# Channel mixing moved ahead of the norm's scale and the pooling, with one load of the input in pairs of chunks

## The chip, the cores and the metric

The kernel runs on one core of one Trainium2 chip. The metric is the device time of one execution in microseconds; before the change it was 927.83 us, the median of 3 runs (927.12 to 928.20). The profile is of one execution of its own, 927.41 us as timed; its span, from the first to the last recorded instruction, is 925.5 us. Engines are named as in the profile: PE (TensorE, matmul), DVE (VectorE), ACT (ScalarE), POOL (GpSimd), SP (SyncE, which issues nearly all loads).

## The reference

A trunk of two layers on 512 tokens with 1024 channels, in float32. Layer 0 mixes tokens by causal pooling, layer 1 by sliding-window attention; each mixer is followed by a gated MLP with a causal convolution of width 3. Only the pooling mixer of layer 0 is touched:

```
def pool_mixer(h, w, b, scale):            # h = rms_norm(x, norm_mix[0])
    ...
    for gi, win in enumerate(POOL_WINDOWS):      # 2, 4, 8, 16
        sl = slice(gi * POOL_GC, (gi + 1) * POOL_GC)   # 256 channels each
        ...
        mean = (c - lo) / count[None, :, None]   # causal mean over win tokens
        outs.append(mean - hf[..., sl])
    p = jnp.stack(outs, axis=2).astype(h.dtype)
    y = jnp.einsum('bsgc,gcd->bsgd', p, w) + b   # one 256x256 matrix per group
    return y.reshape(B, S, D) * scale
...
h = h + pool_mixer(rms_norm(h, norm_mix[0]), ...)
hn = rms_norm(h, norm_ffn[0])
h = h + conv_glu_ffn(hn, ...)
```

Pooling acts on tokens and the 256x256 matrix on channels, so the two commute; the norm's per-channel weight can be folded into the matrix, and its per-token factor r0 can be put on either side of the matrix, but must stand before the pooling.

## The kernel before

The channels lie in NC = 8 chunks of P = 128 partitions, the S = 512 tokens along the free dimension, in NT = 4 tiles of 128. The stream is the eight tiles h[c] (128x512); the f0x tiles are its chunks for the MLP, scaled with that norm's weight. Matrix products keep float32 accuracy by splitting each operand into two float32r parts, h (rounded, by ACT) and l (the rest, by DVE or, for weights called with the engine G, by POOL in quarters of 256 columns). `mm3` makes three matmuls of one product: h by h, l by h, h by l (L84, L85, L86). The eight PSUM banks hold 512 float32 columns each.

`pool_mixer` ran in this order. x came twice. First by tokens (`xt`, 4 loads of 512 KB): ACT squares each token tile and sums it along the row, a short chain on ACT and DVE makes the factor r0 of these tokens, DVE scales a band matrix (128 x 144 columns: the pooling window of a token tile and its spill into the next) with it, and eight plain float32 matmuls (L299) pool the eight channel chunks, straight from `xt`. Then, for every chunk in turn, `mixed` (m) evicts the pooled bank as two float32r parts, `product` (p) multiplies with the mixing matrix (six matmuls with 512 columns), `bias` (b) adds a per-channel bias to h[c], which came transposed in a second set of eight loads, `total` (t) adds the product to h[c] on DVE, and `normed` (n) makes f0x of it: the rounded part on ACT, the rest on DVE (`split_scaled`, L258 and L259). `early_weights` (w) splits the first four tiles of the MLP's input matrix.

A string `order` sets in which sequence these steps are issued; the instructions marked `pin` keep that sequence on their engine. Each engine works its queue strictly in order, and an instruction that waits holds up those behind it. PE's queue has all pooling, then all products, then the MLP.

The MLP (`mlp_in`) starts with two weight tiles together: for each chunk k six matmuls, three for each tile, 48 in all, then the second pair of tiles the same way, then one tile at a time. All that follows is the same in both kernels.

Of the kernel before, what the change touches and what calls it, by code (L numbers as in the profile page):

```python
# [19 lines left out]
F32 = mybir.dt.float32  # L20
F32R = mybir.dt.float32r
# [36 lines left out]
def trunk(ctx: ExitStack, tc: tile.TileContext, x_tok, x_t, vecs, w_pool, w_kq, w_v, w_o, w_in, w_out, out_a, out_b):  # L58
# [10 lines left out]
    def small(pool, n, words, dt=F32, **kw):  # L69
        return pool.tile([P, words], dt, **kw)[:, :n]  # L70
# [72 lines left out]
    xt = fst.tile([P, NT, D], F32, name="xt")  # L143
    for i in range(NT):
        nc.sync.dma_start(xt[:, i, :], x_tok[i * P : (i + 1) * P, :])
    vec = small(cst, NV, -(-NV // 64) * 64, name="vec")
    wpool_raw = [fst.tile([P, 1024], F32, name=f"wpool{g}_raw") for g in range(2)]
    for g in range(2):
        nc.sync.dma_start(wpool_raw[g], w_pool[:, g * 1024 : (g + 1) * 1024])
# [9 lines left out]


# [3 lines left out]
    band = fst.tile([P, 8, BW], F32, name="band")  # L164
    def edge_copy(g):
        a = WINDOWS[g] - 1
        pin(V.tensor_copy(band[:, 4 + g, a:], band[:, g, a:]))

    for g, w in enumerate(WINDOWS):
        b = band[:, g, :]  # L170
        V.memset(b, 1.0 / w)
        G.affine_select(b, b, [[1, BW]], ALU.is_ge, 0.0, base=0, channel_multiplier=-1)
        G.affine_select(b, b, [[-1, BW]], ALU.is_ge, 0.0, base=w - 1, channel_multiplier=1)
        G.affine_select(b, b, [[1, BW]], ALU.not_equal, 1.0 / w - 1.0, base=0, channel_multiplier=-1)
        f = band[:, 4 + g, : w - 1]
        G.affine_select(f, rc[:, : w - 1], [[1, w - 1]], ALU.is_ge, 0.0, base=0, channel_multiplier=-1)
        G.tensor_tensor(f, f, ident[:, : w - 1], ALU.subtract)
        if g < 2:
            edge_copy(g)
    ones = cst.tile([P, P], F32, name="ones")  # L180
    G.memset(ones, 1.0)


    def rsqrt_mean(dst, ssq, n, root=False):
# [7 lines left out]
        if root:  # L192
            A.activation(y, ssq, AF.Sqrt, bias=eps, scale=1.0 / D)
# [68 lines left out]

    def pool_mixer(norm, xs, ws):
        r0 = small(fst, NT, 32, name="r0")
        ss0 = small(fst, 2 * NT, 32, name="ss0")

        warm = small(fst, BW, 192, name="warm")
        V.memset(warm, 0.0)
        for i in range(12):
            T.matmul(banks[-1][:, :BW], lhsT=warm[:, :P], rhs=warm, start=True, stop=True)  # L270
        for i in range(NT):

            cut = D // 2 if i == 0 else D
            junk = fst.tile([P, D], F32, tag="junk", name=f"junk{i}")
            if cut < D:
                pin(
                    V.tensor_tensor_reduce(
                        out=junk[:, cut:],
                        in0=xt[:, i, cut:],
                        in1=xt[:, i, cut:],  # L280
                        scale=1.0,
                        scalar=0.0,
                        op0=ALU.mult,
                        op1=ALU.add,
                        accum_out=ss0[:, NT : NT + 1],
                    )
                )
            A.activation(junk[:, :cut], xt[:, i, :cut], AF.Square, accum_out=ss0[:, i : i + 1])
            if cut < D:
                pin(V.tensor_tensor(ss0[:, i : i + 1], ss0[:, i : i + 1], ss0[:, NT : NT + 1], ALU.add))  # L290
                for g in (2, 3):
                    edge_copy(g)
            rsqrt_mean(r0[:, i : i + 1], ss0[:, i : i + 1], 1, root=True)
            n = min(BW, S - i * P)
            sband = fst.tile([P, 4, BW], F32, tag="sband", name=f"sband{i}", bufs=2)
            e = 0 if i else 4
            pin(V.tensor_scalar(sband[:, :, :n], band[:, e : e + 4, :n], r0[:, i : i + 1], None, ALU.mult))
            for c in range(NC):
                T.matmul(  # L299
                    banks[c][:, i * P : i * P + n],  # L300
                    lhsT=xt[:, i, c * P : (c + 1) * P],
                    rhs=sband[:, c // 2, :n],
                    start=(i == 0),
                    stop=(i == NT - 1),
                    skip_group_check=True,
                )
        wpool = []
        for g in range(4):
            raw = wpool_raw[g // 2][:, (g % 2) * 512 : (g % 2 + 1) * 512]
            hh = fst.tile([P, 512], F32R, name=f"wpool{g}_h")  # L310
            ll = fst.tile([P, 512], F32R, name=f"wpool{g}_l")
            A.activation(hh, raw, AF.Copy)
            pin(V.tensor_tensor(ll, raw, hh.bitcast(F32), ALU.subtract))
            wpool.append((hh, ll))
        pre = [(0, 1), (0, 0), (1, 1), (1, 0)]
        raws = [fetch(w_in[0, j, t], D, f"wi0_{j}_{t}") for j, t in pre[:3]]
        for c in range(NC):
            nc.sync.dma_start(h[c], x_t[:, c, :])
        bs = small(cst, NC, 64, name="bs")
        pin(V.tensor_tensor(bs, vec[:, V_PB : V_PB + NC], vec[:, V_PS : V_PS + NC], ALU.mult))  # L320
        pool_x = {}

        def mixed(c):
            pool_x[c] = split_scaled(banks[c], col(V_NM + c), f"px{c}", pin)
# [18 lines left out]
        def normed(c):  # L343
# [488 lines left out]
```

## Time and profile before

| what | before |
|---|---|
| median of 3 runs | 927.83 us |
| the profiled execution, as timed | 927.41 us |
| its span | 925.5 us |
| mean granted PE clock | 0.998 |
| pooling matmuls (L299) on PE | from 7.69 us |
| products of the mixing matrix on PE | from 15.62 us |
| first MLP matmul on PE | 26.65 us |
| x by tokens: loads, size | 4 of 512 KB |
| x by channels: loads, size | 8 of 256 KB |

Times inside the span count from its first instruction. A group's row gives an engine, an operation, the tiles written and read, the shape, the count, the busy time and the mean duration of one, then the engine's idle time ahead of it and what ended that. A row of the timeline gives start and duration, and "x4" merges four instructions that follow each other. A row of the table by stretch gives the stretch, its length and the busy time and count of PE, of PE's weight loads, of DVE, ACT and POOL, then the granted clock, the share of the DMA engines and GB/s.

### The profile page before, as it was taken

To read this page: it belongs to the slowest core of one execution; us is meant where nothing else is said; L and a number is where in the kernel's file an instruction comes from. 1 tells how busy PE (TensorE), PEld (TensorE's weight loads), DVE (VectorE), ACT (ScalarE), POOL (GpSimd) and SP (SyncE) were. 2 spreads that over 40 slices of the span, in tenths; PEclk is the share of its full clock that TensorE was granted. 3 is DMA by queue.
4 is the path that set the end of the run, shared out by engine and by line. 5 is a ranking of instruction groups with operands and counts; after the bars stand their busy time and mean duration, and the time that the engine had idled before them with its cause. 6 is when DMAs were issued, how large, how long until landed. Compare 5 with 4: busy or idle time off the path is not lost.

```text
span 925.5 us, 11713 instructions
## 1 busy us (share of the span) xinstructions
PE 912.8 (99%) x4419; PEld 769.7 (83%) x4419; DVE 578.4 (62%) x974; ACT 422.1 (46%) x682; POOL 132.3 (14%) x216
## 2 busy tenths in 40 slices
PE   8999999999999999999999999999999999999997
PEld 8888888888888888898888888888888888888896
DVE  7589776336777754455888472987743377677433
ACT  7664443224444433336877351744422244444532
POOL 3800000000000001317765040000000000000022
PEclk9999999999999999999999999999999999999999
DMA  8233322333232233322110041242233422322312
GB/s 334 69 113 116 112 64 80 95 128 114 92 98 102 62 90 104 114 91 91 47 46 24 24 137 56 82 158 86 63 94 100 137 91 95 111 77 64 95 61 91
DMA packets 28855, 88.13 MB, mean 95 GB/s; under 512 B 3200, under 2 KB 4352, under 8 KB 28800
## 3 DMA queue, kind: packets, MB, share of 16 engines
q1 hardware_dynamic: 28800, 87.40, 29.2%
q8 instruction: 34, 0.56, 0.2%
q14 instruction: 21, 0.17, 0.1%
HBM read 85.29 MB, written 2.10 MB: 94 GB/s over the span
## 4 chain that ended last, share of the span: by engine, by line
PE 88%; POOL 3%; DVE 3%; ACT 2%; issue 2%; DMA 1%; SPq 0%; ACTq 0%; POOLq 0%; DVEq 0%
PE bank L84 29%; PE bank L86 29%; PE bank L85 29%; POOL wi_l L101 2%; DMA wi_raw<-w_in 1%; ACT sc L625 1%; PE bank L608 1%; PE bank L638 1%; POOL n_acc L231 1%; DVE q L521 1%; POOL wo_l L101 0%; DVE sc L611 0%; PE bank L248 0%; ACT q L520 0%; DVE wi_l L101 0%
## 5 line engine op out<-in xcount | busy, mean ns | idle before, releaser
L98 ACT ACTIVATE wi_h<-wi_raw 128x1024 fp32r<-128x1024 f32 x88 | 93.0, 1060 | 102.4 <-PE bank L85 97.8
L231 POOL TENSOR_TENSOR n_acc<-n_acc,n_sq 128x512 f32<-128x512 f32 (+1 forms) x28 | 37.1, 1327 | 708.0 <-ACT n_sq L222 701.2
L84 PE MATMUL bank<-f0x_h,wi_h 128*128 128x512 f32 x352 | 137.1, 390 | 0.0
L84 PE MATMUL bank<-f1x_h,wi_h 128*128 128x512 f32 x352 | 137.1, 390 | 0.0
L84 PE MATMUL bank<-zh,wo_h 128*128 128x512 f32 (+1 forms) x363 | 137.0, 378 | 0.0
L86 PE MATMUL bank<-f0x_h,wi_l 128*128 128x512 f32 x352 | 137.0, 389 | 0.0
L86 PE MATMUL bank<-f1x_h,wi_l 128*128 128x512 f32 x352 | 137.0, 389 | 0.0
L85 PE MATMUL bank<-f0x_l,wi_h 128*128 128x512 f32 x352 | 136.9, 389 | 0.0
L85 PE MATMUL bank<-f1x_l,wi_h 128*128 128x512 f32 x352 | 136.9, 389 | 0.0
L86 PE MATMUL bank<-zh,wo_l 128*128 128x512 f32 (+1 forms) x363 | 136.6, 376 | 0.0
L85 PE MATMUL bank<-zl,wo_h 128*128 128x512 f32 (+1 forms) x363 | 136.6, 376 | 0.0
L101 DVE TENSOR_TENSOR wi_l<-wi_raw,wi_h 128x1024 fp32r<-128x1024 f32 x84 | 103.6, 1235 | 50.0 <-ACT wi_h L98 47.3
L98 ACT ACTIVATE wo_h<-wo_raw 128x768 fp32r<-128x768 f32 (+1 forms) x70 | 57.5, 822 | 123.7 <-PE bank L85 111.7
L365 DVE TENSOR_TENSOR c_u<-bank,n_rb 128x512 f32<-128x512 f32 x88 | 60.0, 687 | 76.4 <-PE bank L86 76.4
L101 DVE TENSOR_TENSOR wo_l<-wo_raw,wo_h 128x768 fp32r<-128x768 f32 (+1 forms) x66 | 60.4, 915 | 54.5 <-ACT wo_h L98 54.3
L85 PEld LDWEIGHTS bank<-zl,wo_h 128*128 128x128 f32 x363 | 68.3, 188 | 12.5
L86 PEld LDWEIGHTS bank<-zh,wo_l 128*128 128x128 f32 x363 | 68.3, 188 | 12.4
L84 PEld LDWEIGHTS bank<-zh,wo_h 128*128 128x128 f32 x363 | 68.3, 188 | 12.3
L86 PEld LDWEIGHTS bank<-f1x_h,wi_l 128*128 128x128 f32 x352 | 66.1, 188 | 13.9
L85 PEld LDWEIGHTS bank<-f0x_l,wi_h 128*128 128x128 f32 x352 | 66.1, 188 | 13.8
L85 PEld LDWEIGHTS bank<-f1x_l,wi_h 128*128 128x128 f32 x352 | 66.1, 188 | 13.7
L86 PEld LDWEIGHTS bank<-f0x_h,wi_l 128*128 128x128 f32 x352 | 66.1, 188 | 13.7
(175 smaller groups left out, 1484.5 us busy)
## 6 DMA issues: line engine op xcount, KB each, us to landing
wi_raw<-w_in SPq DMA_DIRECT2D x88, 512.0 KB, 3.2
wo_raw<-w_out SPq DMA_DIRECT2D x31, 384.0 KB, 3.1
wo_raw<-w_out SPq DMA_DIRECT2D x31, 320.0 KB, 2.9
kq_raw<-w_kq SPq DMA_DIRECT2D x10, 512.0 KB, 3.3
wo_raw<-w_o SPq DMA_DIRECT2D x8, 512.0 KB, 3.2
xt<-x_tok SPq DMA_DIRECT2D x4, 512.0 KB, 4.8
h<-x_t SPq DMA_DIRECT2D x8, 256.0 KB, 8.1
wpool_raw<-w_pool SPq DMA_DIRECT2D x2, 512.0 KB, 7.7
```

What stands on the lines that cost most here:

```text
L84: T.matmul(ps, lhsT=wh, rhs=xh, start=start, stop=False, **kw)
L85: T.matmul(ps, lhsT=wh, rhs=xl, start=False, stop=False, **kw)
L86: T.matmul(ps, lhsT=wl, rhs=xh, start=False, stop=stop, **kw)
L98: pin(A.activation(h[:, :n], raw[:, :n], AF.Copy))
L101: (eng or V).tensor_tensor(l[:, o], raw[:, o], h[:, o].bitcast(F32), ALU.subtract)
L231: eng.tensor_tensor(self.acc[:, lo:hi], self.acc[:, lo:hi], sq[:, lo:hi], ALU.add)
L365: V.tensor_tensor(u, ps, rb, ALU.mult)
L521: V.scalar_tensor_tensor(t[dst], u[src], b, t[src].bitcast(F32), ALU.add, ALU.subtract)
L608: T.matmul(o, lhsT=qt, rhs=kt[:, kk : kk + 256], start=x == 0, stop=x == 1)
L625: A.activation(t, t, AF.Exp, bias=neg[:, i : i + 1], scale=-1.0, accum_out=den[:, i : i + 1])
L638: T.transpose(ps[:, i * P : (i + 1) * P], sc[i // 2][:, i % 2, kb * P : (kb + 1) * P], ident)
```

## The change

x is loaded once, by channels, as four pairs of chunks (`h2`, 512 KB each), each followed by its group's mixing matrix (256 KB). A small load on ACT's queue brings the norm's eight weight columns (`gm`). Per group, `scaled` (w) multiplies the mixing matrix with the norm's weight; for group 3 alone it is also split in two parts. `square` (s) adds the squares of the chunks into one tile on ACT and DVE. `mix` (y) multiplies the raw chunks with the scaled matrix, tokens on the output's partitions: plain float32 matmuls with 256 columns for groups 0 to 2, `mm3` for group 3, whose chunks `split` (x) has split. `scales` (r) sums the squares over channels with four matmuls and makes r0 for all 512 tokens at once. `evict` (e) reads a mixed group out of PSUM, times r0, as two float32r parts in four pieces of 256 columns, taken from its two banks in turn. `pool` (c) multiplies these parts with the band matrices, which are now float32r: nine matmuls for a chunk, of 144, 128 and (one) 16 columns. `bias`, `total` and `normed` are as before, but for the bias of chunks 0 and 1, which goes to POOL. 8 warming matmuls instead of 12 stand ahead of it all, and POOL makes the band matrices of float32r parts.

```
-    for i in range(NT):
-        nc.sync.dma_start(xt[:, i, :], x_tok[i * P : (i + 1) * P, :])
...
-    for g in range(2):
-        nc.sync.dma_start(wpool_raw[g], w_pool[:, g * 1024 : (g + 1) * 1024])
+    nc.scalar.dma_start(gm, vecs[:, V_NM : V_NM + NC])
+    for g in range(4):
+        nc.sync.dma_start(h2[g], x_t[:, 2 * g : 2 * g + 2, :])
+        nc.sync.dma_start(wpool_raw[g], w_pool[:, g * 512 : (g + 1) * 512])
     nc.sync.dma_start(vec, vecs)
...
-        for c in range(NC):
-            nc.sync.dma_start(h[c], x_t[:, c, :])
...
+        ONE = (3,)
+        YB = (0, 1, 2, 3, 4, 5, 7, 6)
...
+        def square(c):
+            if c == 0:
+                pin(A.activation(acc, h[c], AF.Square))
+                return
+            sq = fst.tile([P, S], F32, tag="sq0", name=f"sq0_{c}", bufs=4)
+            pin(A.activation(sq, h[c], AF.Square))
+            pin(V.tensor_tensor(acc, acc, sq, ALU.add))
...
+        def mix(g):
+            g, half = divmod(g, 10)
+            for i in (2 * half, 2 * half + 1):
+                ps = banks[YB[2 * g + i // 2]][:, (i % 2) * 256 : (i % 2 + 1) * 256]
+                sl = slice(i * P, (i + 1) * P)
+                for k in range(2):
+                    c = 2 * g + k
+                    if g in ONE:
+                        mm3(ps, tuple(t[:, sl] for t in gx[c]), gw[g][k], k == 0, k == 1)
+                    else:
+                        T.matmul(ps, lhsT=h[c][:, sl], rhs=gw[g][k], start=k == 0, stop=k == 1)
...
+        def scales(_):
+            ps = banks[6]
+            for j in range(NT):
+                T.matmul(ps[:, 2 * j : 2 * j + 2], lhsT=acc[:, j * P : (j + 1) * P], rhs=ones[:, :2], start=True, stop=True)
+            rsqrt_mean(r0, ps[:, : 2 * NT].rearrange("p (a b) -> p a b", b=2)[:, :, 0], NT, root=True)
...
+        def evict(g):
...
+            for i in (0, 2, 1, 3):
+                ps = banks[YB[2 * g + i // 2]][:, (i % 2) * 256 : (i % 2 + 1) * 256]
+                c = r0[:, i : i + 1]
+                pin(A.activation(yh[g][i], ps, AF.Copy, scale=c))
+                pin(V.scalar_tensor_tensor(yl[g][i], ps, c, yh[g][i].bitcast(F32), ALU.mult, ALU.subtract))
...
+        def pool(c):
...
+            for i in range(NT):
+                w = min(BW, S - i * P)
+                b = band if i else edge_h
+                steps = [(y[g][i][:, o : o + P], b[:, g, :w]) for y in (yh, yl)]
+                if i == 0:
+                    steps.append((yh[g][i][:, o : o + P], edge_l[:, g, :]))
...
-            "m0 m1 p0 p1 w0 m2 m3 p2 p3 b0 b1 t0 m4 m5 p4 p5 t1 b2 b3 t2 m6 m7 p6 p7 t3 w1 b4 b5 t4 t5 "
-            "n0 b6 b7 t6 n1 t7 n2 w2 n3 n4 w3 n5 n6 n7"
+            "w0 s0 s1 y0 y1 w1 s2 s3 y10 y11 w2 s4 s5 w3 s6 s7 x6 x7 i0 r0 y20 y21 y30 y31 b0 b1 e0 c0 c1 e1 c2 c3 "
+            "e2 i1 c4 c5 t0 n0 e3 c6 c7 b2 t1 n1 b3 t2 n2 b4 t3 n3 b5 t4 n4 b6 t5 n5 b7 t6 n6 i2 t7 n7 i3"
```

(In the new string w is `scaled`, and i is `early_weights`.)

DVE's queue before, where the last totals (L341, written to h) and the first remainders of f0x (L259) stand:

```order
L341 SCALAR_TENSOR_TENSOR h4_100<-bank4_74,vec_90,h4_100 128x512
L341 SCALAR_TENSOR_TENSOR h5_101<-bank5_75,vec_90,h5_101 128x512
L259 SCALAR_TENSOR_TENSOR f0x0_l_401<-h0_96,vec_90,f0x0_h_400 128x512
L341 SCALAR_TENSOR_TENSOR h6_102<-bank0_70,vec_90,h6_102 128x512
L259 SCALAR_TENSOR_TENSOR f0x1_l_408<-h1_97,vec_90,f0x1_h_407 128x512
L341 SCALAR_TENSOR_TENSOR h7_103<-bank1_71,vec_90,h7_103 128x512
L259 SCALAR_TENSOR_TENSOR f0x2_l_413<-h2_98,vec_90,f0x2_h_412 128x512
L259 SCALAR_TENSOR_TENSOR f0x3_l_424<-h3_99,vec_90,f0x3_h_423 128x512
```

The same queue now, from the end of the third group's evictions on (yl2 and yl3 are groups 2 and 3; h0_95 holds chunks 0 and 1, h1_96 chunks 2 and 3, and so on):

```order
L348 SCALAR_TENSOR_TENSOR yl23_396<-bank5_75,r0_199,yh23_392 128x256
L385 SCALAR_TENSOR_TENSOR h0_95<-bank0_70,vec_99,h0_95 128x512
L269 SCALAR_TENSOR_TENSOR f0x0_l_432<-h0_95,vec_99,f0x0_h_431 128x512
L348 SCALAR_TENSOR_TENSOR yl30_439<-bank7_77,r0_199,yh30_435 128x256
L348 SCALAR_TENSOR_TENSOR yl32_441<-bank6_76,r0_199,yh32_437 128x256
L348 SCALAR_TENSOR_TENSOR yl31_440<-bank7_77,r0_199,yh31_436 128x256
L348 SCALAR_TENSOR_TENSOR yl33_442<-bank6_76,r0_199,yh33_438 128x256
L385 SCALAR_TENSOR_TENSOR h0_95<-bank1_71,vec_99,h0_95 128x512
L269 SCALAR_TENSOR_TENSOR f0x1_l_472<-h0_95,vec_99,f0x1_h_471 128x512
L385 SCALAR_TENSOR_TENSOR h1_96<-bank2_72,vec_99,h1_96 128x512
L269 SCALAR_TENSOR_TENSOR f0x2_l_478<-h1_96,vec_99,f0x2_h_477 128x512
L385 SCALAR_TENSOR_TENSOR h1_96<-bank3_73,vec_99,h1_96 128x512
```

Before, six totals stood ahead of f0x0_l and all eight ahead of f0x2_l; now each total stands behind the f0x remainder of the chunk ahead of it, and chunk 0's comes ahead of the evictions of group 3.

ACT's queue before, from the first rounded part of f0x (L258) on (L338 is the bias, L98 a weight tile):

```order
L258 ACTIVATE f0x0_h_400<-h0_96,vec_90 128x512
L338 ACTIVATE h6_102<-h6_102,bs_292 128x512
L338 ACTIVATE h7_103<-h7_103,bs_292 128x512
L258 ACTIVATE f0x1_h_407<-h1_97,vec_90 128x512
L258 ACTIVATE f0x2_h_412<-h2_98,vec_90 128x512
L98 ACTIVATE wi0_1_1_h_416<-wi0_1_1_raw_282 128x1024
L258 ACTIVATE f0x3_h_423<-h3_99,vec_90 128x512
L258 ACTIVATE f0x4_h_427<-h4_100,vec_90 128x512
```

ACT's queue now at the same place (yh are evictions, L268 the rounded part of f0x, L382 the bias, L238 and L232 the squares for the MLP's norm, L98 a weight tile):

```order
L98 ACTIVATE wi0_0_0_h_405<-wi0_0_0_raw_193 128x1024
L268 ACTIVATE f0x0_h_431<-h0_95,vec_99 128x512
L347 ACTIVATE yh30_435<-bank7_77,r0_199 128x256
L347 ACTIVATE yh32_437<-bank6_76,r0_199 128x256
L238 ACTIVATE n0_acc_526<-h0_95 128x512
L347 ACTIVATE yh31_436<-bank7_77,r0_199 128x256
L347 ACTIVATE yh33_438<-bank6_76,r0_199 128x256
L382 ACTIVATE h1_96<-h1_96,bs_197 128x512
L268 ACTIVATE f0x1_h_471<-h0_95,vec_99 128x512
L382 ACTIVATE h1_96<-h1_96,bs_197 128x512
L232 ACTIVATE n0_sq1_0_528<-h0_95 128x512
L268 ACTIVATE f0x2_h_477<-h1_96,vec_99 128x512
```

Before, the squares stood behind all eight f0x parts and the biases stood in pairs; now a bias and a square stand between two f0x parts.

PE's queue before, at the end of the pooling (L299) and the start of the products:

```order
L299 MATMUL bank6_76<-sband3_252,xt_85 128x128
L299 MATMUL bank7_77<-sband3_252,xt_85 128x128
L84 MATMUL bank0_70<-px0_h_294,wpool0_h_262 128x512
L85 MATMUL bank0_70<-px0_l_295,wpool0_h_262 128x512
L86 MATMUL bank0_70<-px0_h_294,wpool0_l_263 128x512
```

PE's queue now, where the mixing, the statistics (L337, four matmuls with 2 columns) and the switch to group 3 meet:

```order
L332 MATMUL bank5_75<-gw20_234,h2_97 128x256
L332 MATMUL bank5_75<-gw21_236,h2_97 128x256
L337 MATMUL bank6_76<-ones_120,n_acc0_198 128x2 x4
L332 MATMUL bank5_75<-gw20_234,h2_97 128x256
L332 MATMUL bank5_75<-gw21_236,h2_97 128x256
L84 MATMUL bank7_77<-gwh30_244,gxh6_258 128x256
L85 MATMUL bank7_77<-gwl30_245,gxh6_258 128x256
L86 MATMUL bank7_77<-gwh30_244,gxl6_259 128x256
```

Before, no statistics ran on PE here and pooling led; now mixing leads, 22 of its 24 plain float32 matmuls stand ahead of the statistics, the 24 matmuls of group 3 behind them, and pooling after those.

More of the change, by code (lines that the diff above doesn't have):

```diff
@@ L57, in trunk @@
 @with_exitstack
-def trunk(ctx: ExitStack, tc: tile.TileContext, x_tok, x_t, vecs, w_pool, w_kq, w_v, w_o, w_in, w_out, out_a, out_b):
+def trunk(ctx: ExitStack, tc: tile.TileContext, x_t, vecs, w_pool, w_kq, w_v, w_o, w_in, w_out, out_a, out_b):
     nc = tc.nc
@@ L158, in trunk @@
     make_identity(nc, ident)
+    ones = cst.tile([P, P], F32, name="ones")
+    G.memset(ones, 1.0)
     rc = small(fst, 16, 64, name="rc")
@@ L192, in rsqrt_mean @@
         if root:
-            A.activation(y, ssq, AF.Sqrt, bias=eps, scale=1.0 / D)
+            pin(A.activation(y, ssq, AF.Sqrt, bias=eps, scale=1.0 / D))
             pin(V.tensor_scalar(v, ssq, -0.5 / D, -0.5 * EPS, ALU.mult, ALU.add))
@@ L263, in pool_mixer @@
     def pool_mixer(norm, xs, ws):
[L264 to L297, printed above, removed]
-            for c in range(NC):
[L299 to L306, printed above, removed]
@@ L809 @@
     arrays = {
-        "x_tok": x,
         "x_t": x.reshape(S, NC, P).transpose(2, 1, 0),
```

115 lines of the change are left out of this document (73 added, 42 removed).

## The prediction

> **What bounds the kernel now.** I read the page's busy shares first, then the PE timeline at the start, then busy time by stretch.
>
> ```profile
> PE 912.8 (99%) x4419; PEld 769.7 (83%) x4419; DVE 578.4 (62%) x974; ACT 422.1 (46%) x682; POOL 132.3 (14%) x216
> 7.69:15.62 7.93, 7.93 (x64) 7.74 (x64) 6.23 (x22) 6.10 (x13) 0.00 (x0) 1.00 1.02 381
> 15.62:26.65 11.03, 11.03 (x49) 9.12 (x49) 10.02 (x15) 11.03 (x18) 6.16 (x8) 1.00 0.61 230
> 26.65:60.00 33.35, 33.15 (x154) 27.41 (x153) 20.21 (x35) 18.39 (x26) 17.21 (x15) 1.00 0.41 127
> 26.65 0.39 PE L84 MATMUL bank<-f0x_h,wi_h 128*128 128x512 f32 x1
> 37.53 0.39 PE L84 MATMUL bank<-f0x_h,wi_h 128*128 128x512 f32 x1
> ```
>
> PE is busy 912.8 of 925.5 us. The first MLP matmul (its operand is f0x, chunk 0 of the normed stream) starts at 26.65 us, and from there PE has no gap to speak of: 33.15 of the next 33.35 us. The 48 matmuls of the first pair of weight tiles end exactly where the row of 37.53 starts, so one takes 10.88 / 48 = 0.2267 us. Everything behind is the same work in both kernels. So the change is worth what it does to **37.53**, the start of the second weight pair, and whatever gap follows it there.
>
> **When the inputs land.** Loads come in the order of SyncE's queue.
>
> ```profile
> 0.80 1.82 SPq L145 DMA_DIRECT2D xt<-x_tok  x4
> 2.67 1.17 SPq L149 DMA_DIRECT2D wpool_raw<-w_pool  x2
> 4.37 0.63 ACT L288 ACTIVATE junk<-xt 128x512 f32<-128x512 f32 x1 [2.07 <-DMA xt<-x_tok]
> DMA to landing us min/median/max: 7.5/7.7/8.0
> ```
>
> The first 0.52 MB are there at 4.37; the second half of w_pool, issued at about 3.4, lands 8.0 later at 11.4, 3.15 MB in all: 2.63 MB in 7.0 us, 0.375 MB/us. The change puts the same 3.15 MB first, cut finer. At this pace the first weights (0.79 MB) are there at 5.1, the last pair of chunks (2.88 MB) at 10.7, vecs at 12.3, the first w_in tile at 13.7. The 2.1 MB of a second copy of x drop out behind them, on queues that nothing of this stretch waits for.
>
> **The new front, to r0.**
>
> ```profile
> 2.22 5.23 PE L270 MATMUL bank<-warm 128*128 128x144 f32 x24 [2.22 <-DVE warm L268]
> 469.73 1.04 PE L638 MATMUL bank<-ident,sc 128*128 128x128 f32 x8
> 470.52 0.47 PE L84 MATMUL bank<-ax_h,kq_h 128*128 128x512 f32 x1
> 471.29 0.28 PE L608 MATMUL bank<-kh,q 128*128 128x256 f32 x1
> 471.41 0.28 PE L608 MATMUL bank<-kl,q 128*128 128x256 f32 x1
> L237 PE MATMUL bank<-ones,n_acc 128*128 128x2 f32 x28 | 3.3, 239 | 0.0
> L222 ACT ACTIVATE n_sq<-h 128x512 f32<-128x512 f32 x25 | 15.4, 621 | 6.9 <-POOL n_acc L231 6.9
> L313 DVE TENSOR_TENSOR wpool_l<-wpool_raw,wpool_h 128x512 fp32r<-128x512 f32 x4 | 2.5, 684 | 0.0
> L193 ACT ACTIVATE rs_y<-ss,eps 128x1 f32<-128x1 f32 x4 | 1.2, 294 | 0.6 <-DVE ss L290 0.5
> L209 DVE TENSOR_TENSOR rs_t<-rs_y 128x4 f32<-128x4 f32 x9 | 1.5, 163 | 0.2
> 6.85 0.16 DVE L211 SCALAR_TENSOR_TENSOR r<-rs_t,rs_y 128x1 f32<-128x1 f32 x1
> 7.11 0.52 DVE L297 TENSOR_SCALAR sband<-band,r 128x576 f32<-128x576 f32 x1
> ```
>
> A plain fp32 matmul shows as two instructions. Pooling on 144 columns took 7.93 / 32 = 0.248 us each (64 rows in the stretch 7.69:15.62), a transpose of 128 columns (470.52 - 469.73) / 4 = 0.198. No row has fp32 at 256 columns; per column these two give 0.395 to 0.44, and I take 0.45 with its issue (one-pass pace, 0.12 as the two rows of L608 stand apart, is the far end). Mixing starts at 5.1 plus the scaling, 5.45. Ahead of the statistics PE has 22 such matmuls: 22 x 0.45 = 9.9, plus half a microsecond for the first ones, in case PE is still as slow as in its first rows (5.23 / 24 = 0.218 an instruction there, 0.124 later), so 15.8. The sum of squares is ready earlier: last chunks 10.7, two squares of 0.62 and DVE's queue of adds (0.68) give 14.2. Four statistics matmuls at about 0.2 (bound 0.239) and their result: 16.8. Root on ACT 0.29 and five dependent DVE steps of 0.2 (0.16 as an instruction alone, 0.26 from 6.85 to 7.11 where one waits for the other): **r0 at 18.1**. The last mixing (fp32r, 24 x 0.12) ends at 20.4, beside this.
>
> **Evictions and pooling.**
>
> ```profile
> L657 ACT ACTIVATE oh<-bank 128x256 fp32r<-128x256 f32 x16 | 6.0, 373 | 10.5 <-PE bank L86 10.4
> L258 ACT ACTIVATE px_h<-bank,vec 128x512 fp32r<-128x512 f32 x8 | 5.1, 687 | 1.6 <-PE bank L299 1.6
> L251 ACT ACTIVATE n_rb<-bank 128x512 f32<-128x512 f32 x3 | 1.8, 599 | 0.6 <-PE bank L248 0.5
> L533 DVE SCALAR_TENSOR_TENSOR vv<-bank,n_r,vec 128x256 f32<-128x256 f32 x4 | 1.9, 484 | 1.9 <-PE bank L86 1.8
> 14.82 1.41 DVE L259 SCALAR_TENSOR_TENSOR px_l<-bank,vec,px_h 128x512 fp32r<-128x512 f32 x2
> L98 ACT ACTIVATE wi_h<-wi_raw 128x1024 fp32r<-128x1024 f32 x88 | 93.0, 1060 | 102.4 <-PE bank L85 97.8
> 16.39 2.83 POOL L101 TENSOR_TENSOR wi_l<-wi_raw,wi_h 128x256 fp32r<-128x256 f32 x4 [9.77 <-ACT wi_h L98]
> ```
>
> An eviction of 256 columns with a scale column costs ACT 0.373 + (0.687 - 0.599) = 0.46, and DVE 0.484. Instructions in a row start about 0.07 closer than they last (two of 0.746 in 1.41), so four pairs need 4 x 0.41 plus 0.18 in which a bank is not free: 1.82 us. Groups 0 to 2 are through DVE at 18.1 + 0.5 + 3 x 1.82 = 24.1. There DVE takes t0 (the residual total of chunk 0), then ACT f0x0_h, which ends at 25.6; ACT's split of a weight tile (1.06) lies beside t0. Only then comes group 3, four pairs with a square of 0.62 between them on ACT, while DVE has f0x0_l in front: the last ends at 28.2, and DVE starts t1 at **28.15**.
>
> A pooling matmul is fp32r with 144 columns, which no row shows. Bounds: by columns below the 256-column row, 0.12 x 144 / 256 = 0.068; the plain fp32 price, 0.248. I take 0.0735 (columns at the 256-row's pace plus its fixed part), since fp32r rows at 256 and 512 columns (0.12, 0.2267) lie on a line. 64 such are then 4.7 us in pieces of 1.2 behind each group, the last piece ending at 29.1. That is the first f0x matmul, **2.5 us later** than 26.65.
>
> **Then one queue sets the pace.** In the new order DVE has t1, f0x1_l, t2, f0x2_l and so on, strictly in turn, where before six totals stood ahead of f0x0_l.
>
> ```profile
> L341 DVE SCALAR_TENSOR_TENSOR h<-bank,vec,h 128x512 f32<-128x512 f32 x8 | 5.7, 744 | 0.0
> L258 ACT ACTIVATE f0x_h<-h,vec 128x512 fp32r<-128x512 f32 x8 | 5.4, 728 | 0.0
> L259 DVE SCALAR_TENSOR_TENSOR px_l<-bank,vec,px_h 128x512 fp32r<-128x512 f32 x8 | 5.6, 746 | 1.0 <-ACT px_h L258 1.0
> ```
>
> f0x_h needs the total, f0x_l needs f0x_h, and the next total stands behind f0x_l: 0.744 + 0.728 + 0.746 = 2.22 us (the 0.07 that neighbours on DVE overlap and the hops between engines about cancel). ACT's bias and square of other chunks fit in the gaps. PE needs only 6 x 0.2267 = 1.36 us for a chunk, so it waits. f0x7_l is done at 28.15 + 7 x 2.22 = 43.7; five more matmuls put the second weight pair at **44.9 instead of 37.53: 7.3 us**. The same additions made for the kernel before end 0.3 late against its trace, so 7.0.
>
> Two smaller terms. The fourth w_in tile is split by ACT behind f0x7_h; POOL, which splits such a tile in quarters of 256 columns and has the third one until 44.6, has one more add (1.3) and then its first quarter (0.74), done at 46.7. PE asks for that at 44.9 + 5 x 0.2267 = 46.0: 0.7 more, with nothing behind it that wins it back. And POOL's adds of squares collide with f0x_l:
>
> ```profile
> 544.04 1.29 POOL L231 TENSOR_TENSOR n_acc<-n_acc,n_sq 128x512 f32<-128x512 f32 x1 [0.99 <-ACT n_sq L222]
> 544.06 1.82 DVE L259 SCALAR_TENSOR_TENSOR f1x_l<-h,vec,f1x_h 128x512 fp32r<-128x512 f32 x1
> 549.38 0.74 DVE L259 SCALAR_TENSOR_TENSOR f1x_l<-h,vec,f1x_h 128x512 fp32r<-128x512 f32 x1
> 549.48 1.78 POOL L231 TENSOR_TENSOR n_acc<-n_acc,n_sq 128x512 f32<-128x512 f32 x1 [4.15 <-ACT n_sq L222]
> ```
>
> Whichever of the two starts second is longer by about what is left of the other (1.82 against 0.74; 1.78 against 1.29). In the new chain an add begins 1.9 us after its chunk's f0x_h and ends at 3.2; the next f0x_l starts 0.76 into a period of 2.2, at 2.97, so 0.13 per chunk once both have settled (six chunks, 0.8); between nothing and 0.35 for each. The Trainium skill, SBUF — State Buffer, section "SBUF: two separate sides", has an exclusive lock between GpSimd and a DVE instruction with two SBUF inputs, held for the whole instruction, by which the wait is all that is left of the other, 0.8 here; had the two shared bandwidth, it would be half of that, 0.4. The four rows agree with the lock.
>
> The sum: 7.0 + 0.7 + 0.8 = **8.5 us** on the profiled execution's 927.41, so 935.9; the median of the runs shown, 927.83, lies 0.4 above it. I say 936.0. Warming matmuls cost nothing (8 x 0.44 from 1.1 us end at 4.6, before the first weights); POOL's band work is through by about 10 and needed at 20.4; the bias of chunks 0 and 1 on POOL at 13 to 15, needed at 24.
>
> **The rivals.**
>
> (a) PE stays the bound, as 99% suggests: ACT and DVE keep up, and the front is the sum of PE's work: 24 x 0.45 + 0.8 + 24 x 0.12 + 5.2 (pooling with its 8 short ones) = 19.7 from 5.45, so f0x starts at 25.15, 1.5 earlier, and the time is **925.9**. It decides if evictions end by about 19 and a chunk's chain falls below 1.36. Against it: 16 evictions on ACT alone are 16 x 0.373 = 6 us behind r0, and DVE's queue has no other order. 4%.
>
> (b) The 144-column fp32r matmul costs 0.248: 64 of them take 16 us from 20.4, f0x starts at 36.9, all chunks are ready, PE runs dense to 47.8: 10.0 later than the same sum for before, **937.6**. For it: the nearest row by columns. 22%.
>
> (c) PE falls back to its first pace. Those first rows ran at 0.218 an instruction although the granted clock reads 1.00. At the wait for group 3 PE idles 2.6 us (25.3 to 27.8). If that sets it back, a chunk takes up to 2.7 on PE against 2.35 for the chain, 2.5 us in all: **938.4**. No row of before has a gap of that kind, so nothing speaks for it but the start: 6%. The Trainium skill, TensorE: Matmul & The Clock Gate, Part 1, asks for about 3.4 us of idleness before the clock is halved; by that rule a gap of 2.6 leaves the sum at 935.9.
>
> (d) Mixing in fp32 and evictions are cheaper than taken (one pass; 0.37 a piece): r0 at 16.3, t1 1.5 sooner still: 3.3 less, **932.7**. 9%.
>
> **How the numbers follow.** Forecast 59%. Its own spread is the bounds of the collision (nothing to 2.4) and of the evictions, 934 to 938. With (b), (c) and (d) the range is 932.0 to 939.0; outside are (a) and the tails, some 12%. About 0.2% (1.9 us) is what a measurement can tell from no change. (a) sits at its edge: faster 2%, within 3%, slower 95%.
>
> **What would show it.** In the new profile: r0's last step near 18; PE idle between pooling pieces, most before bank 7's; f0x_h rows on ACT about 2.2 to 2.4 us apart, each followed by an f0x_l that waits for it; f0x7's matmuls near 44. The forecast is wrong if f0x rows stand 1.4 apart, if pooling rows are 0.2 apart, or if the first f0x matmul starts before 26.

## The result and the profile after

The changed kernel takes **938.16 us** (937.39 to 940.49, 4 runs) against 927.91 for the kernel before (4 runs): ratio 1.0116, 95% interval 1.0103 to 1.0129. It is slower by 10.2 us. The profiled execution is the slowest of the four, 940.49, so its own loss against the profiled execution of before (927.41) is 13.1.

The page's first line of the changed kernel, and busy time by stretch (each row: stretch, its length, busy time and instructions of PE, PE's weight loads, DVE, ACT and POOL, then the granted TensorE clock, DMA share and GB/s):

```profile
PE 920.7 (98%) x4451; PEld 776.4 (83%) x4451; DVE 580.5 (62%) x971; ACT 424.1 (45%) x688; POOL 139.0 (15%) x230
0.00:6.80 6.80, 3.67 (x17) 3.45 (x17) 2.09 (x23) 2.42 (x5) 5.93 (x32) 1.00 0.64 185
6.80:18.89 12.09, 12.09 (x52) 10.45 (x53) 7.89 (x14) 7.64 (x15) 5.92 (x10) 0.86 0.81 317
18.89:23.47 4.58, 3.99 (x31) 3.71 (x30) 3.30 (x9) 2.24 (x7) 3.06 (x5) 1.00 0.14 27
23.47:31.38 7.91, 6.22 (x54) 6.10 (x55) 6.66 (x15) 6.97 (x16) 3.24 (x4) 1.00 0.15 53
31.38:38.30 6.92, 6.92 (x26) 6.25 (x27) 4.55 (x7) 5.58 (x10) 2.56 (x2) 0.51 0.21 78
```

The clock column is the surprise: 0.86 while PE mixes, 0.51 from 31.4 to 38.3. PE's timeline of the same execution (start, time, instruction; in brackets the idle time before it and what ended it):

```profile
6.80 11.45 PE L332 MATMUL bank<-gw,h 128*128 128x256 f32 x44 [1.97 <-DVE gw L302]
18.08 0.95 PE L337 MATMUL bank<-ones,n_acc 128*128 128x2 f32 x8
31.38 0.40 PE L363 MATMUL bank<-edge_h,yh 128*128 128x144 f32 x1 [1.70 <-DVE yl L348]
35.20 0.73 PE L84 MATMUL bank<-f0x_h,wi_h 128*128 128x512 f32 x1
45.51 0.50 PE L85 MATMUL bank<-f0x_l,wi_h 128*128 128x512 f32 x1 [0.22 <-DVE f0x_l L269]
47.73 0.50 PE L85 MATMUL bank<-f0x_l,wi_h 128*128 128x512 f32 x1 [0.31 <-DVE f0x_l L269]
48.99 0.39 PE L84 MATMUL bank<-f0x_h,wi_h 128*128 128x512 f32 x1
49.90 0.39 PE L85 MATMUL bank<-f0x_l,wi_h 128*128 128x512 f32 x1
51.93 0.50 PE L86 MATMUL bank<-f0x_h,wi_l 128*128 128x512 f32 x1 [1.64 <-POOL wi_l L101]
```

The second weight pair starts at 48.99 instead of 37.53, 11.5 late, and PE then waits for POOL's quarter of the fourth w_in tile (from 49.90 to 51.93 is 1.8 more than one matmul's 0.23). Together that is 13.3, against a loss of 13.1 in this execution: **all of the loss is made before 52 us**. DVE's timeline shows r0's last steps and the beginning of the chain:

```profile
19.92 0.66 DVE L220 TENSOR_TENSOR rs_t<-rs_t,rs_v 128x4 f32<-128x4 f32 x1
20.61 0.65 DVE L221 SCALAR_TENSOR_TENSOR r<-rs_t,rs_y 128x4 f32<-128x4 f32 x1
31.54 0.74 DVE L385 SCALAR_TENSOR_TENSOR h<-bank,vec,h 128x512 f32<-128x512 f32 x1
33.08 0.75 DVE L269 SCALAR_TENSOR_TENSOR f0x_l<-h,vec,f0x_h 128x512 fp32r<-128x512 f32 x1 [0.79 <-ACT f0x_h L268]
33.74 0.74 DVE L385 SCALAR_TENSOR_TENSOR h<-bank,vec,h 128x512 f32<-128x512 f32 x1
35.28 0.80 DVE L269 SCALAR_TENSOR_TENSOR f0x_l<-h,vec,f0x_h 128x512 fp32r<-128x512 f32 x1 [0.79 <-ACT f0x_h L268]
45.37 0.74 DVE L385 SCALAR_TENSOR_TENSOR h<-bank,vec,h 128x512 f32<-128x512 f32 x1
46.91 0.77 DVE L269 SCALAR_TENSOR_TENSOR f0x_l<-h,vec,f0x_h 128x512 fp32r<-128x512 f32 x1 [0.79 <-ACT f0x_h L268]
```

Each f0x_l is preceded by 0.79 us in which DVE waits for ACT, and the next total stands behind it: 2.2 to 2.6 us a chunk. But PE itself waits for f0x_l at only two chunks, since it was slow as well. Two explanations therefore stand side by side: DVE's strict turn, and PE at half its clock. ACT's rows for two of these f0x_h show that ACT, too, had stood idle, until DVE's total was there:

```profile
34.52 0.72 ACT L268 ACTIVATE f0x_h<-h,vec 128x512 fp32r<-128x512 f32 x1 [0.35 <-DVE h L385]
39.40 0.72 ACT L268 ACTIVATE f0x_h<-h,vec 128x512 fp32r<-128x512 f32 x1 [0.77 <-DVE h L385]
```

r0 comes at 21.3 where 18.1 was predicted, a third thing to explain.

### The profile page after: what moved, and what is told of

It is laid out like the page before. It is cut to its first block, busy times and chain, and to the rows that moved or that the text cites. A ratio compares the mean times of both kernels' runs of the same rounds, so it can differ in the third digit from the quotient of the medians.

```text
span 938.7 us, 11796 instructions
## 1 busy us (share of the span) xinstructions
PE 920.7 (98%) x4451; PEld 776.4 (83%) x4451; DVE 580.5 (62%) x971; ACT 424.1 (45%) x688; POOL 139.0 (15%) x230
## 4 chain that ended last, share of the span: by engine, by line
PE 90%; DVE 4%; ACT 3%; POOL 2%; issue 1%; DMA 0%; SPq 0%; ACTq 0%; POOLq 0%; DVEq 0%
PE bank L84 29%; PE bank L86 29%; PE bank L85 29%; PE bank L332 1%; ACT sc L665 1%; PE bank L648 1%; PE bank L678 1%; DVE q L561 1%; ACT f0x_h L268 1%; DVE h L385 1%; DMA wpool_raw<-w_pool 0%; DVE yl L348 0%; POOL wi_l L101 0%; POOL o L780 0%; POOL wo_l L101 0%
## 5 line engine op out<-in xcount | busy, mean ns | idle before, releaser
L98 ACT ACTIVATE wi_h<-wi_raw 128x1024 fp32r<-128x1024 f32 x88 | 92.9, 1059 | 110.3 <-PE bank L85 104.5
L98 ACT ACTIVATE wo_h<-wo_raw 128x768 fp32r<-128x768 f32 (+1 forms) x70 | 57.5, 823 | 123.4 <-PE bank L85 111.6
L84 PEld LDWEIGHTS bank<-f0x_h,wi_h 128*128 128x128 f32 x352 | 66.5, 189 | 14.2 <-ACT f0x_h L268 0.4
```

The costliest lines, as they stand in the source:

```text
L84: T.matmul(ps, lhsT=wh, rhs=xh, start=start, stop=False, **kw)
L98: pin(A.activation(h[:, :n], raw[:, :n], AF.Copy))
```

## The experiments

Eleven kernels were run, each in five rounds (4 to 11 executions) beside the kernel before (927.57 to 927.88 in the three groups). Times are medians; traces are of one execution.

**1. Order or clock: four edits.** The first puts each total ahead of the f0x_l before it:

```diff
-"e2 i1 c4 c5 t0 n0 e3 c6 c7 b2 t1 n1 b3 t2 n2 b4 t3 n3 b5 t4 n4 b6 t5 n5 b7 t6 n6 i2 t7 n7 i3"
+"e2 i1 c4 c5 t0 t1 e3 c6 c7 n0 b2 t2 n1 b3 t3 n2 b4 t4 n3 b5 t5 n4 b6 t6 n5 b7 t7 n6 i2 n7 i3"
```

> Only the order on DVE and ACT changes: t1 stands ahead of group 3's evictions, and from then on the total of chunk c+1 stands ahead of f0x_l of chunk c, so that DVE has work while ACT makes f0x_h. Theory 1 (DVE's strict turn t, wait for f0x_h, f0x_l sets the pace, 2.3 us a chunk in the profile of the changed kernel): the pace falls to what ACT needs (f0x_h, bias and square, 0.63 + 0.63 + 0.55 = 1.8), f0x7_l ends near 43.8, the second weight pair starts near 44.9 in place of 48.99, and the time falls by 4 us to 934. Theory 2 (PE's half pace from 31.4 to 38.3 is a cost of its own): PE then has no slack left, starts f0x at about 34.2, loses 3.1 us to the half pace there and is dense to 46.6: a gain of only 2.4 us, 935.8, and PE shows no wait for f0x_l. No gain at all (938) if neither is the limit.

Measured: **933.55** (1.0063, 1.0051 to 1.0076), 4.6 less. DVE's rows, then busy PE by stretch (busy time, clock, DMA), then three PE rows and the last step of r0:

```profile
31.34 0.74 DVE L385 SCALAR_TENSOR_TENSOR h<-bank,vec,h 128x512 f32<-128x512 f32 x1
32.01 0.74 DVE L269 SCALAR_TENSOR_TENSOR f0x_l<-h,vec,f0x_h 128x512 fp32r<-128x512 f32 x1
38.20 2.28 DVE L269 SCALAR_TENSOR_TENSOR f0x_l<-h,vec,f0x_h 128x512 fp32r<-128x512 f32 x2
```

```profile
29.60:31.30 1.70, 1.70 (x9) 0.50 0.69 280
31.30:34.00 2.70, 2.70 (x7) 0.50 0.00 0
34.00:38.00 4.00, 4.00 (x14) 0.71 0.01 2
```

```profile
28.24 0.31 PE L363 MATMUL bank<-edge_h,yh 128*128 128x144 f32 x1 [0.64 <-DVE yl L348]
44.47 0.39 PE L84 MATMUL bank<-f0x_h,wi_h 128*128 128x512 f32 x1
6.64 9.76 PE L332 MATMUL bank<-gw,h 128*128 128x256 f32 x44 [1.26 <-DVE gw L302]
18.79 0.16 DVE L221 SCALAR_TENSOR_TENSOR r<-rs_t,rs_y 128x4 f32<-128x4 f32 x1
```

DVE now goes at 1.32 us a chunk and is done with f0x at 40.5; PE has no wait left and gets to the second pair at 44.47. So the order was the limit, and once it is gone PE is the limit and the half clock costs time: of the five executions, the one with a mean clock of 0.998 took 931.90, the others (0.993 and 0.994) 933.5 to 933.8. The clock was lost behind a gap of only 0.64 us. Some 1.8 of the 4.6 is the wait for the fourth tile, which is gone too, since ACT reaches that tile earlier. And in this profile r0 is there at 19.0, 2.3 earlier than in the changed kernel's, though the edit does not touch the front: the 44 rows of mixing took 9.76 here and 11.45 there. So the 44.47, close to the 44.9 that was expected, owes about half of its 4.5 us to a better front, which is luck. In the medians the fourth edit below puts the front at 0.6, which leaves an estimated 2.2 us for the order itself.

The second edit only fills the gap ahead of group 3's pooling:

```diff
+        def filler(n):
+            for i in range(n):
+                T.matmul(banks[0][:, :BW], lhsT=warm[:, :P], rhs=warm, start=True, stop=True)
...
-"e2 i1 c4 c5 t0 n0 e3 c6 c7 ...
+"e2 i1 c4 c5 t0 n0 e3 f7 c6 c7 ...
```

> Seven plain fp32 matmuls on the zero tile, 7 x 0.248 = 1.7 us, fill PE's wait ahead of group 3's pooling (29.6 to 31.4); nothing else changes. Both theories expect the granted clock at 1.00 from 31 to 38 and pooling of group 3 at 0.11 a matmul. Theory 1: PE then waits for f0x_l at every chunk instead, the second weight pair still starts near 49, time unchanged, 938.2 within 0.5. Theory 2: the half pace was the cost; the time falls by 2.5 to 3.4 us, to about 935.2.

Measured: **938.73** (1.0121, 1.0106 to 1.0137), no gain. Busy PE by stretch, then PE's rows:

```profile
31.30:34.00 2.70, 2.70 (x22) 1.00 0.59 197
34.00:38.00 4.00, 4.00 (x18) 1.00 0.00 2
```

```profile
38.72 0.50 PE L85 MATMUL bank<-f0x_l,wi_h 128*128 128x512 f32 x1 [0.70 <-DVE f0x_l L269]
47.69 0.50 PE L85 MATMUL bank<-f0x_l,wi_h 128*128 128x512 f32 x1 [0.31 <-DVE f0x_l L269]
```

The clock is whole and PE waits at five chunks in turn instead; the second weight pair starts at 48.95. **The half clock from 31 to 38 cost the changed kernel nothing**; DVE's turn hid it. (The fourth edit agrees: its four executions had mean clocks from 0.994 to 0.998 and lie within 0.2 us.)

> The new order of the totals and the seven filling matmuls together. Theory 1: as with the order alone, 934. Theory 2: the filling gives 2 us more than the order alone, and only with both is PE ready by 44.2, so that ACT's pace sets the end: 934 here against 935.8 there.

The two edits together gave **937.74** (936.07 to 940.52), which neither theory allows. ACT's timeline tells why the run does not answer the question:

```profile
36.35 1.14 ACT L232 ACTIVATE n_sq<-h 128x512 f32<-128x512 f32 x2
38.84 0.63 ACT L232 ACTIVATE n_sq<-h 128x512 f32<-128x512 f32 x1 [1.36 <-POOL n_acc L241]
39.38 0.70 ACT L268 ACTIVATE f0x_h<-h,vec 128x512 fp32r<-128x512 f32 x1
```

The order of the squares is not written out by hand, and here three of them landed ahead of f0x6_h on ACT; a square needs a buffer that POOL's addition must free, so f0x_h waited for POOL. The larger part came behind that: POOL's additions also held up its quarter of the fourth w_in tile, for which PE waited 2.30 us, and then the clock was at half until 52:

```profile
48.19 0.55 PE L86 MATMUL bank<-f0x_h,wi_l 128*128 128x512 f32 x1 [2.30 <-POOL wi_l L101]
```

A confounded run, but it names a hidden queue: the squares had to be placed by hand before the question could be put again (group 2).

The fourth edit is `range(8)` to `range(15)` in the warming loop.

> 15 warming matmuls at the start in place of 8, so that PE works until about 6.5 us and has no gap ahead of mixing. Theory 3 (r0 came 3.2 us later than predicted in good part because PE idled from 4.8 to 6.8 and mixed at a granted clock of 0.5 until 11): mixing of group 0 is through by 10.6, the statistics matmuls start at 16.7 (when the sum of squares is there) in place of 18.1, and all that follows is 1.4 earlier: 936.8. Rival (late weights alone set r0): the clock reads 1.00 from 7 to 11, r0 stays at 21.3, and the time at 938.2.

Measured: **937.55** (937.40 to 937.59; 1.0109). The four executions now agree within 0.2 us, where the changed kernel's spread over 3.1. The statistics and r0's last two steps:

```profile
16.59 1.02 PE L337 MATMUL bank<-ones,n_acc 128*128 128x2 f32 x8 [0.68 <-DVE n_acc L312]
18.42 0.16 DVE L220 TENSOR_TENSOR rs_t<-rs_t,rs_v 128x4 f32<-128x4 f32 x1
18.62 0.16 DVE L221 SCALAR_TENSOR_TENSOR r<-rs_t,rs_y 128x4 f32<-128x4 f32 x1
```

r0 is there at 18.8, 2.5 earlier than in the profile of the changed kernel: 1.5 because the statistics start at 16.59 and not 18.08 (two of the 22 mixing matmuls now stand behind them), the rest because its DVE steps take 0.16 in place of 0.65, being through before POOL splits the first w_in tile (from 18.96; in the changed kernel's profile POOL was at that from 19.14). So the front explains 2.5 of the 3 us between the two profiled executions, but at most 0.6 of the medians. The late front is not in every execution: with eight warming matmuls and nearly the same landing times the profiles have r0 at 21.3 (the changed kernel), 19.0 (new order), 21.2 (filling) and 18.9 (both). What fifteen bring is that the executions agree.

**2. What is left.** All kernels from here on have the 15 warming matmuls, unless said otherwise. First the fourth tile's remainder goes from POOL to DVE, in the same quarters:

```diff
-ws.append(in_weights(0, *pre[i], G, raws[i] if i < 3 else None, pin))
+ws.append(in_weights(0, *pre[i], G if i < 3 else None, raws[i] if i < 3 else None, pin, 256))
```

> The 15 warming matmuls, and besides that only the remainder of the fourth w_in tile moves from POOL to DVE, in the same quarters. Theory 4 (1.7 us of the loss is PE waiting at 47.8 to 49.5 for POOL, which has the third tile and an add of squares in front): DVE is free at 45.2 and ACT has this tile's first half-product ready at 46.8, so the first quarter is there at about 47.2 and PE does not wait: 937.55 - 1.7 = 935.9. Rival (PE would wait next for the tile's load or for ACT): unchanged, 937.5.

Measured: **935.67** (1.0084, 1.0071 to 1.0098), 1.9 below the run with the warming alone. The wait is gone and nothing took its place.

Then the order of the totals again, with the squares for the next norm behind all f0x, added by DVE:

```diff
         for c in range(NC):
-            norm.add(c)
+            norm.add(c, eng=V, pin=pin)
```

> 15 warming matmuls, the new order of the totals, and the squares for the next norm put behind all f0x on ACT, their additions on DVE in place of POOL. Theory 1 in full (the strict turn t, f0x_h, f0x_l, with squares between, is what PE waits for): the two squares between group 3's evictions go, t, f0x_h and f0x_l follow each other at DVE's 1.32 a chunk, below PE's 1.36, and PE alone sets the end. If PE keeps its full clock: group 3 evicted at 26.6, pooled by 28.9, 48 matmuls of 0.2267 to 39.8, 2.3 later than before: 930. If PE drops to half pace at about 29.6 even without a gap (its pooling rows being too short to count as full work): 3 us more, as with the order alone, 932 to 933. Rival to theory 1: 935 or more.

Measured: **930.58** (1.0032, 1.0020 to 1.0045). Busy time by stretch, then a row of PE:

```profile
23.00:29.00 6.00, 6.00 (x57) 6.00 (x55) 5.57 (x13) 5.20 (x11) 2.81 (x4) 1.00 0.22 85
29.00:34.00 5.00, 5.00 (x30) 4.32 (x29) 5.00 (x8) 5.00 (x9) 0.00 (x0) 1.00 0.32 107
```

```profile
41.19 0.39 PE L84 MATMUL bank<-f0x_h,wi_h 128*128 128x512 f32 x1
```

In this profile there is no gap and no loss of clock, and 7.6 of the 10.2 us are back (0.6 of them by the warming) without touching what is computed. The run changes several things at once; the squares without the new order were not tried. The rows of the changed kernel speak against the squares as the main cause, since ACT was idle for 0.35 and 0.77 us ahead of f0x_h, waiting for the total. POOL's late quarter needs no care here: with i2 and i3 further ahead and the squares off POOL it is in time.

> The kernel with the late squares, and six filling matmuls (1.5 us) ahead of group 3's pooling. If PE dropped to half pace in it, the filling keeps the clock at 1.00 and the time falls by up to 1.5 (3 less the 1.5 for the filling itself); if it kept its clock, the time rises by 0.5 to 1.5, since PE has no gap there left to fill.

With six filling matmuls (`e3 f6 c6 c7`) this became **931.87**, 1.3 more: PE had kept its clock, so the filling only adds work.

**3. Is PE's own work what remains?** Three attempts at the last 2.7 us. The squares and the statistics earlier on ACT and DVE:

```diff
-"... w2 s4 s5 w3 s6 s7 x6 x7 i0 r0 y20 y21 y30 y31 b0 b1 e0 c0 c1 ...
+"... w2 s4 s5 s6 s7 w3 r0 x6 x7 b0 b1 y20 y21 y30 y31 e0 i0 c0 c1 ...
```

> The kernel with the late squares, and on ACT and DVE the last two squares and the statistics ahead of group 3's splits, ACT's split of the first w_in tile behind group 0's evictions. Theory 5 (with the queues in order PE's own work is the floor: 24 mixing matmuls of 0.45 from 6.6, statistics 0.8, group 3's 24 of 0.12, 64 pooling matmuls of 0.11 and 8 short ones, 8.1, and 48 of 0.2267 make 40.1 against 37.53 before): 930.3, still 2.5 above the kernel before, however early r0 is. Rival (r0 and the evictions are the limit): r0 comes 1.5 earlier than 18.8 and the time is 1.5 below that of the late squares, about 928.5.

**930.83**: r0 at 17.9 instead of 18.8, and no gain. The evictions no longer follow it, as gxl and the moved weight split stand between them. r0 alone was not the limit; PE's floor of 40.1 is not reached either (41.56).

Then 32 pooling matmuls, those of the remainders yl, were left out (the remainders are made as before, the output lacks their part):

> The kernel with the late squares, with the 32 pooling matmuls of the remainders yl left out (the remainders are still made, so the evictions are the same; the output lacks their part). Theory 5 (what is left above the kernel before is PE's own work): PE loses 32 x 0.11 = 3.5 us of work, of which the evictions and the chain let 1.5 to 2.5 through: 928 to 929. Rival (evictions, not PE, hold the start of f0x): PE only waits more, 930.5.

Measured: **932.67**, 2.1 *more* with less work. Busy time by stretch, and PE's row ahead of group 3:

```profile
23.00:29.00 6.00, 4.06 (x30) 3.84 (x30) 5.57 (x13) 5.20 (x11) 2.79 (x4) 0.77 0.23 81
29.00:34.00 5.00, 5.00 (x18) 4.14 (x18) 5.00 (x8) 5.00 (x9) 0.00 (x0) 0.59 0.32 105
```

```profile
27.75 0.46 PE L363 MATMUL bank<-edge_h,yh 128*128 128x144 f32 x1 [1.82 <-DVE yl L348]
42.37 0.39 PE L84 MATMUL bank<-f0x_h,wi_h 128*128 128x512 f32 x1
```

Group 3 can be pooled only when it is evicted: f0x starts at 29.9 against 30.2. The work taken away became gaps, the clock fell in them (0.77, then 0.59), and the f0x matmuls paid for it: the second pair starts 1.2 later (42.37 against 41.19). The other 0.9 of the 2.1 arises at the end of this profile: out_b is stored 2.83 us after PE's last rows in place of 1.96, as DVE's last scale waits there for POOL's output work; whether the other executions share that is not known. Neither expectation had the lost clock.

The third starts PE earlier: 12 warming matmuls, `s6 s7` ahead of `w3`, and the statistics behind all mixing (`y20 y21 r0`).

> The kernel with the late squares, but 12 warming matmuls in place of 15 (PE free at 6.2 in place of 7.9), the last two squares ahead of group 3's weight split, and the statistics behind all 24 mixing matmuls. Theory 5 in its plain form (PE's sum alone): PE starts mixing 1 to 1.6 earlier and everything follows, 929.3. Rival (group 3 is pooled when it is evicted, and the evictions hang on r0, which stays at 19): 930.6, with a new wait of 1 us ahead of pooling.

**932.30**, scattered from 930.53 (clock 0.998) to 933.94 (0.993). In the profiled execution, the slowest, PE reached group 3 early, waited 0.53 and had its clock at about 0.5 from 29 to 36; the other four have no trace, but their times fall as their mean clocks rise. In the fastest, with 0.998, the time is that of the late squares, as the rival said. Two runs in a row thus say that the evictions hold group 3. So they were made cheaper, from the same start: y is kept in fp32, one eviction a piece, half on ACT and half on DVE, with plain fp32 pooling.

```diff
-                pin(A.activation(yh[g][i], ps, AF.Copy, scale=c))
-                pin(V.scalar_tensor_tensor(yl[g][i], ps, c, yh[g][i].bitcast(F32), ALU.mult, ALU.subtract))
+                if i < 2:
+                    pin(A.activation(yh[g][i], ps, AF.Copy, scale=c))
+                else:
+                    pin(V.tensor_scalar(yh[g][i], ps, c, None, ALU.mult))
```

> As the run with the earlier start, but y is kept in fp32 in one piece: 16 evictions shared between ACT and DVE in place of 32, and 32 pooling matmuls in plain fp32 (0.248 each, 7.9 us in all) in place of 64 in fp32r with 8 short ones (8.1). If the evictions hold the start of f0x: group 3 is there at 25, PE is dense from 6.3 (10.5 + 0.85 + 2.9 + 7.9), f0x starts at 28.5 and the second weight pair at 39.4, 1.8 earlier than with the late squares: 928.8. If PE's pooling price is higher than taken, or the queue of t and f0x binds: 930 or more.

Measured: **928.73** (1.0014, 1.0005 to 1.0024). PE has no wait between 6.68 and the end of the first pair:

```profile
6.68 10.63 PE L328 MATMUL bank<-gw,h 128*128 128x256 f32 x48 [0.22 <-DVE gw L298]
20.91 0.41 PE L358 MATMUL bank<-edge,y 128*128 128x144 f32 x2
28.49 0.48 PE L84 MATMUL bank<-f0x_h,wi_h 128*128 128x512 f32 x1
39.49 0.39 PE L84 MATMUL bank<-f0x_h,wi_h 128*128 128x512 f32 x1
```

Here PE is dense, and what it has to do is 28.49 - 6.68 = 21.8 us ahead of f0x; in the kernel before the same part, from its first pooling at 7.69 to 26.65, was 19.0. **That difference of 2.8, less the 1.0 by which PE starts earlier, is, at these prices, the floor of this form**, and the 1.2 us still lost on the time (39.49 is 2.0 late, some 0.8 of which comes back later, 0.6 of it in two waits of PE that are shorter: 0.8 in place of 1.2 for the attention's q, none in place of 0.2 at the norm's statistics). No version beat the kernel before.

## Why the prediction was right, and where it was off

936.0 was forecast and 938.16 came; the sign and the mechanism were right, the size was 2.2 short, just outside the forecast's own spread of 934 to 938 and inside the range. The run with fifteen warming matmuls, 0.6 below the median, shows where a usual execution misses: 1.1 at the fourth w_in tile, 0.7 at r0, and the 0.3 that the forecast took off because the same sum came out late for the kernel before (some 0.7 comes back behind 52 us). By its steps, in the profiled execution (8.5 forecast, 13.1 found):

- **r0 at 18.1** came at 21.3: 3.2 of the missing 4.6. The price of mixing was right (22 matmuls were taken at 0.45; in the kernel with the late squares 20 take from 7.90 to 16.65, 0.4375 each). Two terms failed. The landing pace: 0.375 MB/us puts the last of the 3.15 MB at 11.4, and the last piece of w_pool came at 13.4 (ACT's wait for it ends there), so that the additions of squares, which stand behind those weights in ACT's and DVE's queues, ended at 16.6, not 14.2. And the warming, put at nothing: the eight matmuls ended at 4.8, two microseconds before mixing, which then ran at half clock until 11, and that, not the landing, held the statistics here. The new order's profile, with the same landing and a gap of 1.26, mixed at full pace and had r0 at 19.0. With PE kept warm r0 came at 18.8, within 0.7 of the forecast.
- **Evictions of 1.82 a group, t1 10.05 behind r0**: measured 1.81 (ACT's rows for groups 1 and 2 start at 22.33 and 24.14) and 31.54 - 21.26 = 10.28. Right.
- **The 144-column fp32r matmul, 0.0735**: mis-sized. The 54 rows of groups 0 to 2, from 23.47 to 29.5, take 0.112 each (the few shorter ones among them included), and those of group 3, at half clock, 0.21. The bounds held it. It did not show in the time since the evictions pace pooling; it does show as soon as PE is the limit, as 64 x 0.0385 = 2.5 us of the floor.
- **The chain t, f0x_h, f0x_l, 2.22 a chunk plus 0.13 for collisions**: from t1 to the end of f0x7_l forecast 16.35, measured 47.68 - 31.54 = 16.14. That this is the cause is shown by the new order, with which DVE goes at 1.32 and PE waits for no f0x_l: together with the squares and their additions out of the way it brought 5.1 us (935.67 to 930.58, the fourth tile's wait being absent from both, r0 at 18.9 and 18.8), against nothing for the filling of PE's gap.
- **The fourth w_in tile, 0.7**: measured 1.8, and 1.9 came back when its remainder was made on DVE. The addition of squares stood in front on POOL, as forecast, so that the first quarter began only when PE asked for it. The sum had 0.74 for that quarter; it took 1.71, since DVE was making the next tile's remainder and POOL had to wait (POOL's rows in the timeline of the changed kernel, then DVE's):

```profile
48.93 1.28 POOL L241 TENSOR_TENSOR n_acc<-n_acc,n_sq 128x512 f32<-128x512 f32 x1
50.17 1.71 POOL L101 TENSOR_TENSOR wi_l<-wi_raw,wi_h 128x256 fp32r<-128x256 f32 x1
```

```profile
49.41 1.88 DVE L101 TENSOR_TENSOR wi_l<-wi_raw,wi_h 128x1024 fp32r<-128x1024 f32 x1 [1.74 <-ACT wi_h L98]
```

- **Rival (c), PE falling back to half pace at the wait for group 3**: it happened, in the place named, and the forecast had given it 6% and 2.5 us. It cost nothing in this kernel, because the chain was slower still, so the time of 938.16 next to the 938.4 of this rival is chance; terms that add up in a sum can hide each other on the chip. 6% was too little for what happened in all six profiles with a gap left open there. The Trainium skill, TensorE: Matmul & The Clock Gate, Part 1, has the clock halved after an idle window of about 3.4 us; the traces here show about 0.5 after gaps of 0.53, 0.64, 1.70 and 1.97 us and do not agree with it as a limit for a single gap.
- **Rival (a), PE as the bound**: its sum put f0x at 25.15. With the measured 0.112 and a start at 6.7 it is 29; the fp32 version reached 28.49. By these prices even perfect queues could not have made this form faster, and the 4% were generous.

The loss of 10.2 by what brought it back: 0.6 the front, 1.9 the fourth tile, 5.1 the order of totals and squares (from 935.67 to 930.58), 1.9 what the last run changed together (undivided evictions on two engines, plain fp32 pooling, PE's start and the place of the statistics), the earlier start alone having brought nothing; about 1 stays, which the sum above puts down to PE's work.

## What to carry to other kernels

Where two engines hand a chunk back and forth (here DVE, ACT, DVE), write the order so that the next chunk's first step stands ahead of this one's last: the same instructions took 1.32 instead of 2.3 us a chunk. Count the work moved onto the bound engine at measured prices before anything else; here it had 21.8 us to do, in the cheapest form tried, where 19.0 had been. And look at the granted clock wherever the bound engine gets short waits: taking 3.5 us of work from PE started the second weight pair 1.2 later.

## What the runs showed of the hardware that was not expected

- In all six profiles with an open PE gap ahead of group 3 (0.53, 0.60, 0.60, 0.64, 1.70 and 1.82 us, behind short pooling matmuls) the clock fell to 0.50 and stayed there for about 7 us. With the gap filled, or absent, it read 1.00. Gaps of 0.68, 0.94 and 1.08 us behind the plain fp32 mixing left it at 1.00 (the run with fifteen warming matmuls alone, late squares with filling, squares and statistics earlier). And it can fall after PE has resumed: with the new order PE was back at 28.24, and the clock read 1.00 from 28 to 29, 0.75 from 29 to 30, then 0.50. So the length of one gap does not decide; whether the shortness of the rows before it does was not separated.
- It differs from execution to execution of one kernel: five of the run with the earlier start went from 930.53 at a mean clock of 0.998 to 933.94 at 0.993, and one of the late squares took 931.94 at 0.996, where four took 930.50 to 930.61.
- Two DVE steps on 128x4 elements took 0.66 and 0.65 us while POOL split a weight tile, 0.16 without. The Trainium skill, SBUF — State Buffer, section "SBUF: two separate sides", has a lock that the one that starts second waits for; the rows beside the split agree, and show that an instruction on 128x4 elements pays the wait too. But POOL's addition of the bias to a chunk, which reads SBUF as well, ran from 15.01 to 18.99 in the run with fifteen warming matmuls, and the same two steps took 0.16 in the middle of it: beside that instruction the lock does not show.
- A stationary operand of 128 columns and a moving one of 144 in fp32r took 0.112 us, more than columns alone would give (0.068, from 0.12 at 256); plain fp32 on 144 columns took 7.58 / 32 = 0.237, so that splitting y into two fp32r halves (64 such) bought PE nothing: 7.2 us and 8 short ones against 7.6.
